# Transposing half of a stage's input by DMA instead of TensorE, at six places of a decoder trunk

## The chip, the cores and the metric

The kernel runs on one core of one Trainium2 chip. The metric is the device time of one execution in microseconds; lower is better.

## The reference

A decoder trunk of two layers on one sequence of 256 tokens, with 1024 features in float32. Each layer has a gated feed-forward network (FFN, 2816 hidden units), a token mixer and a second FFN. The first layer's mixer is a recurrent block, the second's is attention over keys and values that are computed once, from the residual between the layers. Every sub-layer has a norm in front and one behind:

```python
for layer in range(DEPTH):
    if layer == N_A_LAYERS:
        k, v, c = shared_kv(h, kv_norm_g, w_kv, w_fgate, b_fgate)
    f = swiglu(rms_norm(h, ffn1_pre_g[layer]), ...)
    h = h + 0.5 * rms_norm(f, ffn1_post_g[layer])
    hn = rms_norm(h, mix_pre_g[layer])
    m = recurrent_block(hn, ...) if layer < N_A_LAYERS else forgetting_attention(hn, w_q, w_o, k, v, c)
    h = h + rms_norm(m, mix_post_g[layer])
    f = swiglu(rms_norm(h, ffn2_pre_g[layer]), ...)
    h = h + 0.5 * rms_norm(f, ffn2_post_g[layer])
```

## The kernel before

**Blocks and units.** The 256 tokens are two blocks of 128, `t` = 0 and 1; the residual of a block is the tile `h[t]`, tokens on the partitions. All weights stream from memory through one list of units (`items`). A unit has a preparation, which loads the weights on SP's queue into one of five `raw` buffers and splits them into an upper and a lower float32r part (`split`: `whi` on ScalarE at L173, `wlo` on VectorE at L177, nine buffers of each), and a work part, once for each block, which is six matmuls of 512 columns for most units. A product is made of three matmuls, upper by upper, lower by upper and upper by lower, of weights and operands (L428, L429 and L432 in `proj_items`; L183 to L185 in `mm3`).

**Order.** TensorE's order is written by hand: `run` lets block 0 go up to seven units ahead of block 1. At the end of a stage block 0 finishes first, block 1 then does its last seven units alone, and block 0 starts the next stage with seven units alone. Each work part ends in a `tick`. `defer(n, fn)` calls `fn` at the (n+1)th tick from there, and so fixes where its TensorE instructions stand. The other engines' order is chosen at compile time from estimated readiness and priority; `tc.high_priority()` puts instructions forward, and `tc.keep_in_program_order` forbids one to stand before what was written ahead of it on its engine.

**From one stage to the next.** When a block's last product of a stage is done, `enter` takes the squares' sums (L205), multiplies by the norm's gain (L284), gets the reciprocal root on GpSimd (L198, L200) and adds to the residual in two halves of 512 features (L297). Then, `wait` ticks later, `inputs` makes the next stage's operand: `to_tp` transposes 128 x 128 tiles of the residual on TensorE (L226), four to a PSUM bank, two banks for eight feature tiles ("k tiles" 0 to 7); `to_x` multiplies them by the next norm's gain into `xg` (L234, VectorE), copies that rounded to the upper part `xhi` (L235, ScalarE) and takes the rest as the lower part `xlo` (L240, VectorE). `stat` takes the squares' sum of the new residual; the norm's factor itself is applied to the products later. The next stage's first unit uses k tiles 0 and 1, its second 2 and 3, its third 4 and 5.

`enter` is called at five changes of stage for both blocks. One makes its operand in another way (`normed`). Four use `inputs`: after the recurrent block, after the first layer's second FFN (where it makes two operands, `dests_l1`: one for the second layer's first FFN, one for the keys and values, whose names begin with z), after the second layer's first FFN, and after attention. After the last FFN nothing follows.

**Transposing transfers that are there already.** The hidden units of the FFN are transposed by DMA: `post_up` copies the float32 tile on GpSimd into two planes of 16-bit halves (L527), `hidden_T` issues a transposing DMA on SP's queue (L535) and a second copy on GpSimd joins the halves again (L540). The helpers `planes`, `swap` and `join` (L212, L216, L220) do the same for keys, queries and gates.

Of the kernel before, what the change touches and what calls it, by code (L numbers as in the profile page):

```python
# [9 lines left out]
F32 = mybir.dt.float32  # L10
# [7 lines left out]
P = 128  # L18
# [25 lines left out]
def trunk_kernel(ctx: ExitStack, tc: tile.TileContext, A: dict, out: bass.AP):  # L44
# [36 lines left out]
    def defer(n, fn):  # L81
        pend.append([n, fn])
# [146 lines left out]
    def x_upper(tp, dest, n):  # L229

        gi, xh, xl = dest
        xg = hpool.tile([P, 4, P], F32, tag="t1", name=nm("xg"), bufs=2)
        g = gT[:, gi + 4 * n:gi + 4 * n + 4].unsqueeze(2).to_broadcast([P, 4, P])
        nc.vector.tensor_tensor(xg, tp.rearrange("p (a b) -> p a b", a=4), g, ALU.mult)  # L234
        nc.scalar.activation(xh[:, 4 * n:4 * n + 4, :], xg, AF.Copy)  # L235
        return xg

    def x_lower(xg, dest, n):
        gi, xh, xl = dest
        nc.vector.tensor_tensor(xl[:, 4 * n:4 * n + 4, :], xg, xh[:, 4 * n:4 * n + 4, :].bitcast(F32), ALU.subtract)  # L240

    def to_x(tps, dest):

        with tc.high_priority():
            xg = [x_upper(tps[n], dest, n) for n in range(2)]
            for n in range(2):
                x_lower(xg[n], dest, n)

    def to_x_tiles(tps, dest):

# [15 lines left out]
    def stat(t):  # L266
        ss = new_ss()
        square_sum(h[t], ss[:, 0:1])
        rs[t] = rstd_of(ss, 1)

    def enter(t, dests, pf, gb, half, last=False, normed=False, wait=3):

        f = 1.0 / 16 if half else 1.0 / 32
        ss = new_ss()
        t1 = []
        urgent = tc.high_priority()
        urgent.__enter__()
        for n in range(2):
            square_sum(pf[n], ss[:, n:n + 1], f)
        for n in range(2):  # L280
            if n == 1 and last:
                r = rstd_of(ss, 2, f, nc.vector)
            t1.append(hpool.tile([P, 512], F32, tag="t1", name=nm("t1"), bufs=2))
            nc.vector.tensor_tensor(t1[n], pf[n], gb[:, n * 512:(n + 1) * 512], ALU.mult)  # L284
        if not last:
            r = rstd_of(ss, 2, f)

        sp, aq = nc.sync, nc.scalar
        pieces = [(n * 512, 512, None) for n in range(2)]
        if last:  # L290
            pieces = ([(0, 1024, sp)] if t == 0 else
                      [(0, 256, sp), (256, 256, aq), (512, 256, sp), (768, 256, aq)])
        for c, m, q in pieces:
            hn = h[t][:, c:c + m]
            for a in range(c, c + m, 512):
                n = min(m, 512)
                nc.vector.scalar_tensor_tensor(h[t][:, a:a + n], t1[a // 512][:, a % 512:a % 512 + n], r[:, 0:1],  # L297
                                               h[t][:, a:a + n], ALU.mult, ALU.add)
            if last:
                q.dma_start(out[0, t * P:(t + 1) * P, c:c + m], hn)  # L300
        urgent.__exit__(None, None, None)
        if last:
            return

        def inputs():
            tps = [to_tp(h[t], n) for n in range(2)]
            for dest in dests:
                to_x(tps, dest)
            stat(t)

        def norm():
            with tc.high_priority():
                normed_x()

        def normed_x():
            ss = new_ss()
            for n in range(2):
                square_sum(h[t][:, n * 512:(n + 1) * 512], ss[:, n:n + 1])
            rs[t] = rstd_of(ss, 2)
            hn = []  # L320
            for n in range(2):
                hn.append(hpool.tile([P, 512], F32, tag="t1", name=nm("hn"), bufs=2))
                nc.vector.tensor_scalar(hn[n], h[t][:, n * 512:(n + 1) * 512], rs[t][:, 0:1], None, ALU.mult)

            def go():
                tps = []
                for n in range(2):
                    tp = gtbank()
                    for j in range(4):
                        nc.tensor.transpose(tp[:, j * P:(j + 1) * P], hn[n][:, j * P:(j + 1) * P], ident)  # L330
                    tps.append(tp)
                to_x_tiles(tps, dests[0])
            defer(6, go)

        if normed:
            norm()
            settled[0] = True
        else:
            defer(wait, inputs)

    def gain_bcast(src):
        gb = hpool.tile([P, D], F32, tag="gb", name=nm("gb"), bufs=1)
# [149 lines left out]
    def ahead(i, fn):  # L492
# [5 lines left out]
            return prep()  # L498
        items[i] = (both, work)

    def ffn_items(pool_of, wg, wu, wd, post_g, next_dests, last=False, normed=False):
        hid = {}
        sil = {}
        box = {}

        def hid_tiles(t):
            if t not in hid:
                hid[t] = (pool_of().tile([P, 22, P], F32R, tag=f"hhi{t}", name=nm("hhi"), bufs=1),
                          pool_of().tile([P, 22, P], F32R, tag=f"hlo{t}", name=nm("hlo"), bufs=1))
            return hid[t]  # L510

        def post_gate(c0, nn):
            def f(t, ps):
                s = pool_of().tile([P, 512], F32, tag="sil", name=nm("sil"), bufs=2)
                nc.scalar.activation(s[:, :nn], ps, AF.Silu, scale=rs[t][:, 0:1])  # L515
                sil[t] = s
            return f

        def post_up(c0, nn):
            def f(t, ps):  # L520
                hh, hl = hid_tiles(t)
                s = sil[t][:, :nn]
                pr = pool_of().tile([P, 512], F32, tag="prod", name=nm("prod"), bufs=2)
                nc.vector.scalar_tensor_tensor(pr[:, :nn], ps, rs[t][:, 0:1], s, ALU.mult, ALU.mult)  # L524
                halves = hpool.tile([P, 512], F32, tag="t1", name=nm("pl"), bufs=2).bitcast(U16)[:, :2 * nn]
                turned = pr.bitcast(U16)[:, :2 * nn].rearrange("p (a b) -> p a b", b=P)
                nc.gpsimd.tensor_copy(halves.rearrange("p (h f) -> p h f", h=2),  # L527
                                      pr[:, :nn].bitcast(U16).rearrange("p (f h) -> p h f", h=2))
                defer(2, lambda: hidden_T(halves, turned, hh, hl))

            def hidden_T(halves, turned, hh, hl):

                m, k0 = nn // P, c0 // P
                keep = tc.keep_in_program_order
                keep(nc.sync.dma_start(turned, halves, transpose=True))  # L535
                hv = hh[:, k0:k0 + m, :].rearrange("p a b -> p (a b)")
                lv = hl[:, k0:k0 + m, :].rearrange("p a b -> p (a b)")

                def join():
                    nc.gpsimd.tensor_copy(halves.rearrange("p (f h) -> p h f", h=2),  # L540
                                          turned.rearrange("p (h a) b -> p h (a b)", h=2))

                def parts():
                    x = halves.bitcast(F32)
                    keep(nc.scalar.activation(hv, x, AF.Copy))  # L545
                    keep(nc.vector.tensor_tensor(lv, x, hv.bitcast(F32), ALU.subtract))  # L546
                defer(3, join)
                defer(7, parts)
            return f

        i0 = len(items)
        for i in range(5):
            proj_items(wg, i * 512, 512, main_x, post_gate(i * 512, 512))
            proj_items(wu, i * 512, 512, main_x, post_up(i * 512, 512))

        last_up = post_up(2560, 256)

        def post_both(t, pg, pu):
            post_gate(2560, 256)(t, pg)
            last_up(t, pu)  # L560

        pair_items(wg, wu, 2560, 256, main_x, post_both)

        def load_gb():
            box["gb"] = gain_bcast(post_g)

        ahead(i0 + 24, load_gb)

        def post_down(t, accs):
            enter(t, next_dests(t), accs, box["gb"], True, last, normed)  # L570

        row_items(wd, [P] * 22, lambda t, k: (hid[t][0][:, k, :], hid[t][1][:, k, :]), post_down, 4 if last else 2)
        return i0

# [644 lines left out]
    def post_q(n):  # L1219
        return lambda t, ps: heads_T(ps, t, n, HD ** -0.5, att["q"][t])  # L1220

    for n in range(2):
        proj_items(A["attn_w_q"][0], n * 512, 512, main_x, post_q(n))
    n_q[0] = len(items)
    row_items(A["attn_w_o"][0], [P] * 8, lambda t, k: (att["oh"][t][:, k, :], att["ol"][t][:, k, :]),
              lambda t, accs: enter(t, [main_dest(GI[("ffn2", 1)], t)], accs, gbox["mix1"], False, wait=4),
              rows0=1, late=True)
    ahead(n_q[0] + 2, load_gb("mix1", A["mix_post_g"][1]))
    n_att = len(items)
# [240 lines left out]
```

## Time and profile before

| | us |
|---|---|
| median of three runs | 965.7 |
| lowest and highest | 965.55, 965.88 |
| the profiled execution | 965.92 |
| its span, first to last instruction | 964.2 |
| TensorE busy | 955.9 |
| VectorE busy | 640.7 |
| ScalarE busy | 527.6 |
| GpSimd busy | 218.2 |

The granted clock of TensorE is 0.999 of full speed. Busy times are unions over one engine's instructions; the profile calls TensorE's matmuls PE and its weight loads PEld, VectorE DVE, ScalarE ACT, GpSimd POOL and the queue of SP SPq. Matmuls overlap each other in the pipeline, so the start of the next one tells more than the length of one. A row of the timeline gives the start and the duration in us, the engine, the line, the operation, the tiles written and read, their shapes, how many instructions are merged, and in brackets what ended the engine's idle time.

### The profile page before, as it was taken

The numbers are of one execution on the slowest core, as the hardware profiler recorded it, in microseconds if no ns is written. First come the engines' busy times: TensorE is split into PE (matmuls) and PEld (weight loads), VectorE is DVE, ScalarE is ACT, GpSimd is POOL, SyncE is SP. The second block draws the span as 40 slices with busy tenths as digits, with TensorE's granted clock in tenths as the row PEclk, the third lists the DMA queues.
The fourth block names the chain that finished last, engine by engine and source line by source line (L and its number), as shares of the span: only waits on it lengthen the run. The fifth ranks groups of instructions, "written<-read, shape, count | busy, mean of one in ns | idle before, by whom it ended". The sixth has DMA issues, their size and how long they took to land.

```text
span 964.2 us, 12866 instructions
## 1 busy us (share of the span) xinstructions
PE 955.9 (99%) x4575; PEld 791.3 (82%) x4575; DVE 640.7 (66%) x845; ACT 527.6 (55%) x750; POOL 218.2 (23%) x221
## 2 busy tenths in 40 slices
PE   9999999999999999999999999999999999999997
PEld 6888888898878888888898888888887788888886
DVE  6658674678997666664686566665488876666642
ACT  7546453568886555443565455444366855444431
POOL 2712330130001323230003522234022012232200
PEclk9999999999999999999999999999999999999999
DMA  8787995475346787775558979878773468777731
GB/s 286 226 258 225 256 284 197 142 228 163 119 123 219 209 236 211 205 242 196 135 182 278 253 219 258 230 216 265 226 256 97 133 199 236 207 222 233 223 109 44
DMA packets 148934, 198.79 MB, mean 206 GB/s; under 512 B 67166, under 2 KB 85958, under 8 KB 148742
## 3 DMA queue, kind: packets, MB, share of 16 engines
q1 hardware_dynamic: 146182, 191.06, 65.6%
q0 software_dynamic: 2080, 6.38, 2.1%
q8 instruction: 36, 0.59, 0.2%
q10 hardware_dynamic: 608, 0.53, 0.2%
q14 instruction: 28, 0.23, 0.1%
HBM read 182.19 MB, written 3.16 MB: 192 GB/s over the span
## 4 chain that ended last, share of the span: by engine, by line
PE 95%; DVE 2%; ACT 1%; issue 1%; POOL 0%; DMA 0%; POOLq 0%; DVEq 0%; ACTq 0%
PE mm L428 16%; PE mm L429 16%; PE mm L432 16%; PE mm L183 13%; PE mm L185 13%; PE mm L184 13%; PE gt L795 2%; PE mm L1305 1%; PE mm L190 1%; PE mm L191 1%; PE mm L192 1%; PE gt L226 1%; ACT pe L1181 1%; DVE wlo L177 0%; PE tr L127 0%
## 5 line engine op out<-in xcount | busy, mean ns | idle before, releaser
L177 DVE TENSOR_TENSOR wlo<-raw,whi 128x1024 fp32r<-128x1024 f32 (+5 forms) x329 | 418.0, 1276 | 230.7 <-ACT whi L173 228.3
L173 ACT ACTIVATE whi<-raw 128x1024 fp32r<-128x1024 f32 (+5 forms) x329 | 341.9, 1045 | 308.6 <-PE mm L432 119.2
L428 PE MATMUL mm<-whi,xhi 128*128 128x512 f32 x656 | 256.6, 391 | 0.0
L429 PE MATMUL mm<-wlo,xhi 128*128 128x512 f32 x656 | 255.5, 389 | 0.0
L432 PE MATMUL mm<-whi,xlo 128*128 128x512 f32 x656 | 202.1, 389 | 0.0
L428 PEld LDWEIGHTS mm<-whi,xhi 128*128 128x128 f32 x656 | 123.2, 188 | 25.9 <-issue 0.7
L432 PEld LDWEIGHTS mm<-whi,xlo 128*128 128x128 f32 x656 | 123.1, 188 | 25.8 <-DVE xlo L240 0.2
L429 PEld LDWEIGHTS mm<-wlo,xhi 128*128 128x128 f32 x656 | 123.2, 188 | 25.4 <-DVE wlo L177 0.3
L183 PE MATMUL mm<-whi,hhi 128*128 128x512 f32 x352 | 137.2, 390 | 0.0
L185 PE MATMUL mm<-whi,hlo 128*128 128x512 f32 x352 | 137.0, 389 | 0.0
L184 PE MATMUL mm<-wlo,hhi 128*128 128x512 f32 x352 | 136.9, 389 | 0.0
L540 POOL COPY pl<-prod 128x1024 uint16<-128x1024 uint16 (+1 forms) x48 | 69.9, 1456 | 174.4 <-DMA prod<-pl 174.4
L527 POOL COPY pl<-prod 128x1024 uint16<-128x1024 uint16 (+1 forms) x48 | 66.3, 1382 | 151.9 <-DVE prod L524 86.8
L183 PEld LDWEIGHTS mm<-whi,hhi 128*128 128x128 f32 x352 | 66.1, 188 | 13.7
L185 PEld LDWEIGHTS mm<-whi,hlo 128*128 128x128 f32 x352 | 66.1, 188 | 13.7
L184 PEld LDWEIGHTS mm<-wlo,hhi 128*128 128x128 f32 x352 | 66.1, 188 | 13.6
L198 POOL TENSOR_SCALAR nv<-ss 128x1 f32<-128x1 f32 x22 | 9.6, 437 | 268.7 <-ACT junk L205 268.7
L524 DVE SCALAR_TENSOR_TENSOR prod<-mm,rstd,sil 128x512 f32<-128x512 f32 (+1 forms) x48 | 33.8, 703 | 29.5 <-PE mm L432 25.9
L515 ACT ACTIVATE sil<-mm,rstd 128x512 f32<-128x512 f32 (+1 forms) x48 | 31.0, 649 | 32.9 <-PE mm L432 25.0
L546 DVE TENSOR_TENSOR hlo<-pl,hhi 128x512 fp32r<-128x512 f32 (+1 forms) x48 | 41.2, 858 | 3.7 <-ACT hhi L545 3.7
L183 PE MATMUL mm<-whi,xhi 128*128 128x512 f32 (+1 forms) x112 | 42.8, 382 | 0.0
L185 PE MATMUL mm<-whi,xlo 128*128 128x512 f32 (+1 forms) x112 | 42.5, 379 | 0.0
(223 smaller groups left out, 1054.6 us busy)
## 6 DMA issues: line engine op xcount, KB each, us to landing
raw<-in_ffn_w_down_dram SPq DMA_DIRECT2D x88, 512.0 KB
raw<-in_ffn_w_up_dram SPq DMA_DIRECT2D x80, 512.0 KB
raw<-in_ffn_w_gate_dram SPq DMA_DIRECT2D x78, 512.0 KB
raw<-in_rg_w_in_dram SPq DMA_DIRECT2D x10, 504.0 KB
raw<-in_rg_w_out_dram SPq DMA_DIRECT2D x10, 504.0 KB
raw<-in_ffn_w_gate_dram SPq DMA_DIRECT2D x19, 256.0 KB
raw<-in_ffn_w_up_dram SPq DMA_DIRECT2D x16, 256.0 KB
raw<-in_rg_w_in_dram SPq DMA_DIRECT2D x8, 512.0 KB
```

What stands on the lines that cost most here:

```text
L173: up = nc.scalar.activation(hi[:parts, c:c + m], rawv[:, c:c + m], AF.Copy)
L177: nc.vector.tensor_tensor(lo[:parts, c:c + m], rawv[:, c:c + m], hi[:parts, c:c + m].bitcast(F32), ALU.subtract)
L183: nc.tensor.matmul(ps, xh, wh, start=first, stop=False)
L184: nc.tensor.matmul(ps, xh, wl, start=False, stop=False)
L185: nc.tensor.matmul(ps, xl, wh, start=False, stop=last)
L428: nc.tensor.matmul(ps, get_x(t, k)[0], u.hi[:, c], start=k == 0, stop=False)
L429: nc.tensor.matmul(ps, get_x(t, k)[0], u.lo[:, c], start=False, stop=False)
L432: nc.tensor.matmul(ps, get_x(t, k)[1], u.hi[:, c], start=False, stop=k == nk - 1)
L524: nc.vector.scalar_tensor_tensor(pr[:, :nn], ps, rs[t][:, 0:1], s, ALU.mult, ALU.mult)
L527: nc.gpsimd.tensor_copy(halves.rearrange("p (h f) -> p h f", h=2), pr[:, :nn].bitcast(U16).rearrange("p (f h) -> p h f", h=2))
L540: nc.gpsimd.tensor_copy(halves.rearrange("p (f h) -> p h f", h=2), turned.rearrange("p (h a) b -> p h (a b)", h=2))
L546: keep(nc.vector.tensor_tensor(lv, x, hv.bitcast(F32), ALU.subtract))
```

## The change

At six of the eight uses of `inputs` the second half of the residual (k tiles 4 to 7) is transposed by a transposing DMA: after the recurrent block for block 1, after the first layer's second FFN for both blocks, after the second layer's first FFN for block 0, and after attention for both. `enter` copies the half into planes (`planes`, GpSimd) as soon as the residual is added. `inputs` transposes only the first half on TensorE, sets the first half of the first operand, and issues the transfer (`swap`, SP); `join` (GpSimd) follows at the next tick, and one tick after that (two for block 1) `turned_to_x` sets the second half: the product with the gain on VectorE and the upper part on ScalarE, both kept in program order, and the lower part. A second operand (keys and values) is set three ticks later, both halves. For block 1 at these places `inputs` comes one tick later than before.

The scratch tiles are old product tiles of the FFN (block 0 behind an FFN), the query tile of block 0 (behind attention), and for block 1 one of the two `t1` tiles and the tile that takes the squares in `stat` (`junk`).

```diff
     def to_x(tps, dest):
         with tc.high_priority():
-            xg = [x_upper(tps[n], dest, n) for n in range(2)]
-            for n in range(2):
-                x_lower(xg[n], dest, n)
+            xg = [x_upper(tp, dest, n) for n, tp in enumerate(tps)]
+            for n, v in enumerate(xg):
+                x_lower(v, dest, n)
+
+    def turned_to_x(v, tps, dests, more):
+        for i, dest in enumerate(dests):
+            def place(i=i, dest=dest):
+                gi, xh, xl = dest
+                if i:
+                    to_x(tps, dest)
+                with tc.high_priority():
+                    xg = (v if i == len(dests) - 1 else more()).rearrange("p (a b) -> p a b", a=4)
+                    g = gT[:, gi + 4:gi + 8].unsqueeze(2).to_broadcast([P, 4, P])
+                    tc.keep_in_program_order(
+                        nc.vector.tensor_tensor(xg, v.rearrange("p (a b) -> p a b", a=4), g, ALU.mult))
+                    tc.keep_in_program_order(nc.scalar.activation(xh[:, 4:, :], xg, AF.Copy))
+                    x_lower(xg, dest, 1)
+            if i:
+                defer(2, place)
+            else:
+                place()
...
+        by_transfer = not normed and (spare or t == 1) and not (half and len(dests) == 1 and t == 1)
+        if by_transfer:
+            a = spare() if t == 0 else hpool.tile([P, 512], F32, tag="t1", name=nm("hp"), bufs=2)
+            with tc.high_priority():
+                planes(a.bitcast(U16), h[t][:, 512:])
+
         def inputs():
-            tps = [to_tp(h[t], n) for n in range(2)]
-            for dest in dests:
+            tps = [to_tp(h[t], n) for n in range(1 if by_transfer else 2)]
+            for dest in dests[:1] if by_transfer else dests:
                 to_x(tps, dest)
             stat(t)
+            if by_transfer:
+                b = spare() if t == 0 else spool.tile([P, 512], F32, tag="junk", name=nm("ht"), bufs=1)
+                with tc.high_priority():
+                    swap(b.bitcast(U16), a.bitcast(U16))
+                defer(0, lambda: join(a.bitcast(U16).rearrange("p (f h) -> p h f", h=2), b.bitcast(U16)))
+                defer(1 + t, lambda: turned_to_x(a, tps, dests, spare))
...
-            defer(wait, inputs)
+            defer(wait + (by_transfer and t), inputs)
...
+    def old_products():
+        return pools["f"].tile([P, 512], F32, tag="prod", name=nm("hp"), bufs=2)
...
+    q_parts = [1, 0]
+
+    def old_q():
+        return att["q"][0].rearrange("p a b -> p (a b)").rearrange("p (s f) -> p s f", s=2)[:, q_parts.pop(), :]
```

`spare=old_products` is passed behind the FFNs and `spare=old_q` behind attention; the recurrent block's call passes none.

More of the change, by code (lines that the diff above doesn't have):

```diff
@@ L269, in stat, with enter @@
         rs[t] = rstd_of(ss, 1)
-    def enter(t, dests, pf, gb, half, last=False, normed=False, wait=3):
+    def enter(t, dests, pf, gb, half, last=False, normed=False, wait=3, spare=None):
         f = 1.0 / 16 if half else 1.0 / 32
@@ L569, in post_down @@
         def post_down(t, accs):
-            enter(t, next_dests(t), accs, box["gb"], True, last, normed)
+            enter(t, next_dests(t), accs, box["gb"], True, last, normed, spare=old_products)
         row_items(wd, [P] * 22, lambda t, k: (hid[t][0][:, k, :], hid[t][1][:, k, :]), post_down, 4 if last else 2)
@@ L1225, in trunk_kernel @@
     row_items(A["attn_w_o"][0], [P] * 8, lambda t, k: (att["oh"][t][:, k, :], att["ol"][t][:, k, :]),
-              lambda t, accs: enter(t, [main_dest(GI[("ffn2", 1)], t)], accs, gbox["mix1"], False, wait=4),
+              lambda t, accs: enter(t, [main_dest(GI[("ffn2", 1)], t)], accs, gbox["mix1"], False, wait=4,
+                                    spare=old_q),
               rows0=1, late=True)
```

## The prediction

> **What bounds the kernel now.** I read the page first, then the waits of TensorE, then the instructions grouped by form, and last the timeline around each place that is changed.
>
> ```profile
> span 964.2 us, 12866 instructions
> ...
> PE 955.9 (99%) x4575; PEld 791.3 (82%) x4575; DVE 640.7 (66%) x845; ACT 527.6 (55%) x750; POOL 218.2 (23%) x221
> ...
> PE 95%; DVE 2%; ACT 1%; issue 1%; POOL 0%; DMA 0%; POOLq 0%; DVEq 0%; ACTq 0%
> ```
>
> TensorE is busy for 99% of the span and carries 95% of the chain that ended last. Busy matmul time overlaps, so I also ask what TensorE ever waited for:
>
> ```profile
> PE tr L127 <- PEq L1455: 0.8, 1, 0.8
> PE gt L795 <- issue: 0.8, 1, 0.8
> PE gt L1165 <- POOL qT L220: 0.3, 1, 0.3
> ```
>
> That is 1.9 us in three waits, none of them at the six places. So a TensorE instruction that goes is worth its full step, and a new wait of TensorE costs its full length. The other engines matter only when they are late.
>
> **Part one: what is removed.** Each of the six places loses four of its eight transposes, 24 of these 64 (group view: number, busy us, mean ns of one, idle before).
>
> ```profile
> L226 PE MATMUL gt<-ident,h 128*128 128x128 f32 x64 | 8.3, 272 | 0.0
> ```
>
> ```profile
> 303.67 0.39 PE L429 MATMUL mm<-wlo,xhi 128*128 128x512 f32 x1
> 303.90 0.62 PE L432 MATMUL mm<-whi,xlo 128*128 128x512 f32 x2
> 304.36 1.03 PE L226 MATMUL gt<-ident,h 128*128 128x128 f32 x8
> 305.15 0.48 PE L428 MATMUL mm<-whi,xhi 128*128 128x512 f32 x1
> ```
>
> The eight in a group start in a pipeline: they last 1.03 us together, each 0.272, so they step by (1.03 - 0.272)/7 = 0.108 us. Four fewer save 0.43 us, and six places save 24 x 0.108 = 2.6 us. The other end comes from the group's busy time, 8.3/64 = 0.130 us, which gives 3.1 us; that counts the group's run-out too, which stays, so I take 2.6. [...]
>
> VectorE's and ScalarE's instructions stay the same in number and size:
>
> ```profile
> L234 DVE TENSOR_TENSOR xg<-gt,gT 128x512 f32<-128x512 f32 x20 | 12.8, 683 | 0.1
> ...
> L235 ACT ACTIVATE xhi<-xg 128x512 fp32r<-128x512 f32 x16 | 9.8, 631 | 4.3 <-DVE xg L234 4.3
> ```
>
> The second half's product with the gains (L234) now reads SBUF instead of PSUM. I price that at nothing: the weight split in a row below reads two SBUF operands of twice the length in 1226 ns, 613 for this length against 683.
>
> **Part two: what is added.** Per place there are a de-interleaving copy on GpSimd, a transposing transfer on SP's queue and a re-joining copy on GpSimd: 12 copies and six transfers. The kernel already does the same for the hidden units, and one such case reads:
>
> ```profile
> 315.36 1.04 POOL L527 COPY pl<-prod 128x1024 uint16<-128x1024 uint16 x1 [8.62 <-DVE prod L524]
> 320.04 1.36 POOL L540 COPY pl<-prod 128x1024 uint16<-128x1024 uint16 x1 [3.64 <-DMA prod<-pl]
> ```
>
> ```profile
> 316.42 1.24 SPq L535 DMA_TRANSPOSE prod<-pl  x1
> ```
>
> ```profile
> POOL pl L540 <- DMA prod<-pl: 174.4, 46, 10.1
> ```
>
> From the residual's end the second half needs 1.04 (copy) + 0.02 + 3.62 (316.42 to 320.04) + 1.36 (copy) + 0.68 + 0.63 = 7.35 us until its upper part can be used. The waits for landing average 174.4/46 = 3.8, and the longest was 10.1. Against this stands the room, from the second half of the residual to the first matmul on k tile 4, which is the third unit of the next stage (units of two k tiles, six matmuls). In order of the six places, each residual pair with the matmul that follows:
>
> ```profile
> 303.10 1.42 DVE L297 SCALAR_TENSOR_TENSOR h<-t,rstd,h 128x512 f32<-128x512 f32 x2 [0.31 <-POOL rstd L200]
> 316.13 0.39 PE L428 MATMUL mm<-whi,xhi 128*128 128x512 f32 x1
> 473.20 1.41 DVE L297 SCALAR_TENSOR_TENSOR h<-t,rstd,h 128x512 f32<-128x512 f32 x2 [0.36 <-POOL rstd L200]
> 484.31 0.39 PE L428 MATMUL mm<-whi,xhi 128*128 128x512 f32 x1
> 484.44 1.40 DVE L297 SCALAR_TENSOR_TENSOR h<-t,rstd,h 128x512 f32<-128x512 f32 x2
> 495.53 0.39 PE L428 MATMUL mm<-whi,xhi 128*128 128x512 f32 x1
> 701.11 1.41 DVE L297 SCALAR_TENSOR_TENSOR h<-t,rstd,h 128x512 f32<-128x512 f32 x2 [0.38 <-POOL rstd L200]
> 712.19 0.39 PE L428 MATMUL mm<-whi,xhi 128*128 128x512 f32 x1
> ```
>
> ```profile
> 779.82 1.42 DVE L297 SCALAR_TENSOR_TENSOR h<-t,rstd,h 128x512 f32<-128x512 f32 x2 [0.24 <-POOL rstd L200]
> 793.40 0.39 PE L428 MATMUL mm<-whi,xhi 128*128 128x512 f32 x1
> ```
>
> The rooms are 316.13 - 304.52 = 11.6, 484.31 - 474.61 = 9.7, 495.53 - 485.84 = 9.7, 712.19 - 702.52 = 9.7 and, for the last place, 793.40 - 781.24 = 12.2; the fifth place, not shown, is block 0 of the same stage as the sixth, and I treat it like that one. Each room shrinks by the 0.43 saved in front of it, so three places have 9.3 against 7.35: a margin of 1.9. In front of the second half there can stand one weight split on VectorE, 1.2 (1226 ns in a row below), and one on ScalarE, 1.3 (an estimate, twice L235's 0.63 for twice its length). With both, the second half comes 9.85 us after the residual, 0.55 late. With a landing slower by 0.2 (3.8 for 3.6) and two copies of 1.54 for 1.04 and 1.36 (rows below), the sum is 10.7 and 1.4 late. So a tight place costs between nothing and 1.4 us; I take 0.17, near the lower end, because the plain chain fits with 1.9 to spare and the new instructions have priority over the splits: 0.5 us over three places. The first, fifth and sixth places I cost at nothing: their room is 2 to 2.5 us longer, which covers the 1.4.
>
> **Part three: what is moved.** The second block's transposes come one unit later, at its three places. What covers this is the rest of the run of block 0's units in between; a unit is 1.4 us (six steps of 0.23, from 303.67 to 303.90), and the group then lasts 0.272 + 3 x 0.108 = 0.6 instead of 1.03. I cost it at nothing, and at 0 to 0.5 per place if VectorE is late. It also gains something: a residual that VectorE finishes late no longer meets TensorE at once. The keys' and values' operands are set later; their first use is four units after.
>
> **Part four: what is queued behind the new waits.** On SP the six transfers wait for their first copy, and weight loads stand behind: 1.24 us each plus the wait. The loads run ahead of their use by five buffers, so this is hidden. On GpSimd the joining copy waits for the landing, and behind it stands the row statistic of the next block. On VectorE and ScalarE the gain product and the upper part are pinned in program order; behind them stand the weight splits, the evictions and the next block's residual. The stage where this hurts is the entry to the second layer, with both blocks and two sets of operands:
>
> ```profile
> 474.50:494.00 19.50, 19.50 (x103) 16.95 (x102) 19.31 (x29) 13.63 (x24) 2.95 (x6) 1.00 0.46 142
> ```
>
> ```profile
> 491.00 0.86 DVE L177 TENSOR_TENSOR wlo<-raw,whi 128x680 fp32r<-128x680 f32 x1
> 494.61 0.31 PE L183 MATMUL mm<-whi,zhi 128*128 128x340 f32 x1
> ```
>
> VectorE (the third pair) is busy 19.31 of 19.50 us there. The first split of 680 columns ends at 491.86, and its first matmul is at 494.61: the weights are 2.75 us ahead. The change puts four copies of GpSimd into this stretch, and they slow VectorE. Two windows of the by-form view, the first without copies, the second with 13:
>
> ```profile
> L177 DVE TENSOR_TENSOR wlo<-raw,whi 128x1024 fp32r<-128x1024 f32 x10 | 12.3, 1226 | 14.6 <-ACT whi L173 14.6
> ```
>
> ```profile
> L177 DVE TENSOR_TENSOR wlo<-raw,whi 128x1024 fp32r<-128x1024 f32 x27 | 36.2, 1339 | 17.9 <-ACT whi L173 17.5 <-DMA raw<-in_ffn_w_up_dram 0.4
> ...
> L527 POOL COPY pl<-prod 128x1024 uint16<-128x1024 uint16 x7 | 10.7, 1532 | 28.8 <-ACT hhi L545 17.9 <-DVE prod L524 11.0
> ...
> L540 POOL COPY pl<-prod 128x1024 uint16<-128x1024 uint16 x6 | 9.3, 1546 | 21.4 <-DMA prod<-pl 21.4
> ```
>
> 27 splits lost 113 ns each, 3.1 us over 13 copies: 0.23 us of VectorE for a copy, 0.9 us for four, inside the 2.75. [...]
>
> **The sum** is made against the profiled execution's 965.9 us (span 964.2 and 1.7 around it): 2.6 saved, 0.5 given back, 2.1 net, 963.8. That execution lies 0.2 above the median of 965.7, so against the median it is **963.6 us**.
>
> **The rivals.** *The second half is late.* Each tight place loses the 1.4 us of the upper bound: 965.7 - 2.6 + 4.2 = 967.3; with half of it, 965.2. For it speaks the margin of 1.9, which two splits ahead use up; against it the priority.
>
> *VectorE stands still and the weights run out (the slower side).* The pinned product waits at the head of VectorE's queue. At the second place it is queued two units behind the transposes, so 2.8 us or more after the residual, while the joining copy ends 1.04 + 0.02 + 3.62 + 1.36 = 6.04 after it: VectorE may idle up to 3.2 us. The third place can do the same, 6.4 together, and 0.9 for the copies makes 7.3. It decides once this passes the lead of 2.75: TensorE then waits up to 4.6 us, and the time is 965.7 - 2.6 + 4.6 = 967.7, or 971.9 with the 4.2 of the late halves on top. For it speaks the 19.31 of 19.50; against it that VectorE's order is chosen by readiness as the compiler expects it, and that the second block's operands for the keys and values now come later, which takes 4 x 0.68 = 2.7 us out of the tight stretch.
>
> [...]
>
> *The change does not do what it says*: the transposes taken out might have filled time in which TensorE would wait anyway. The 1.9 us of waits lie elsewhere, so 2 in 100; the time would be 965.7.
>
> **How the numbers follow.** A measurement of this kernel can tell about 0.2%, 1.9 us, from no change: 963.8 and 967.6 are the bounds. The forecast has 0.52 and ends below 963.8. The late second half has 0.22, and lies within the bounds. The stand-still has 0.20 and lies past 967.6. Exclusion has 0.04 and no effect 0.02, both within. So faster 0.52, same 0.28, slower 0.20. The range runs from 962.9, with 2.6 saved and nothing given back, rounded down by the spread of the runs, to 967.5, which leaves out the stand-still.
>
> **What would show it.** In the changed profile L226 would have 40 matmuls instead of 64, the groups at the six places four each; GpSimd 12 more copies of about 1.0 to 1.5 us; the transposing transfers six more at about 1.24. TensorE's waits would stay near 1.9 us, or show the upper part (the place's ScalarE line) at k tile 4 for the late half, and weight splits (L177) in the second layer's entry for the stand-still. I am wrong on the first term if the groups of four take more than about 0.6 us, and on the second if any of the three tight places shows TensorE waiting for more than 1 us.

## The result, and the profile after

| | before | after |
|---|---|---|
| median of six runs, us | 965.71 | 970.65 |
| lowest and highest, us | 965.55, 966.06 | 969.74, 973.3 |
| mean granted clock of TensorE in the runs | 0.998 to 1.0 | 0.995 to 0.997 |

The changed kernel is slower: after to before 1.0052, 95% interval 1.0041 to 1.0062. It takes 4.9 us more, where the forecast had 2.1 us less. The time lies above the forecast's range and inside the slower rival's 967.7 to 971.9, but that is chance: the rival is added up from waits of TensorE for late weights and for the late halves, and the trace below has 0.3 us of these. The execution that was profiled is the slowest of the six (973.3). Of the 7.4 us by which its span is longer, 1.9 lie ahead of every changed place: its first transposes of the residual (L226) start at 298.36, before at 296.47.

The head of the page of the changed kernel and its chain (columns as before):

```profile
span 971.6 us, 12835 instructions
...
PE 958.9 (99%) x4551; PEld 792.0 (82%) x4551; DVE 647.9 (67%) x845; ACT 527.5 (54%) x750; POOL 244.5 (25%) x233
...
PE 91%; DVE 2%; ACT 2%; issue 2%; DMA 1%; POOL 1%; POOLq 0%; ACTq 0%; DVEq 0%
```

TensorE is as good as always busy in both, and lost 24 instructions, yet its busy time is 3 us longer (958.9 for 955.9): some of its matmuls got longer. The chain gave 4 points of TensorE to other engines, so there are new waits. TensorE's waits in the changed kernel (total us, times, longest):

```profile
PE mm L183 <- ACT zhi L235: 2.0, 1, 2.0
PE gt L226 <- DVE h L316: 0.9, 2, 0.5
PE gt L829 <- issue: 0.8, 1, 0.8
PE tr L127 <- PEq L1495: 0.8, 1, 0.8
PE mm L1345 <- DVE whi L1312: 0.5, 1, 0.5
PE mm L463 <- DVE xlo L240: 0.3, 1, 0.3
PE gt L1199 <- POOL qT L220: 0.2, 1, 0.2
```

Of the waits over 0.2 us, the two of 0.8 were there before. The one of 0.5 for `whi` L1312 lies in the kernel's first unit, ahead of every place changed. It belongs to this execution rather than to the change: one variant below shows no such wait, another one of 0.8. The other three rows, 3.2 us, are new, and they lie at two of the four changes of stage: 2.4 us come from the entry to layer 2's first FFN, where both blocks have a transfer (L183 and one of the two for L226), and 0.9 from the change of stage behind that FFN, where only block 0 has one (L463 and the other for L226). Each has its row below.

Four groups of instructions, by form (busy us, mean ns, idle before):

```profile
L212 POOL COPY hp<-h 128x1024 uint16<-128x1024 uint16 x5 | 9.5, 1895 | 7.6 <-DVE h L316 7.6
L226 PE MATMUL gt<-ident,h 128*128 128x128 f32 x40 | 6.0, 276 | 1.0 <-DVE h L316 0.9
...
L260 DVE TENSOR_TENSOR hp<-hp,gT 128x512 f32<-128x512 f32 x7 | 4.8, 689 | 8.9 <-POOL hp L220 8.9
...
L261 ACT ACTIVATE xhi<-hp 128x512 fp32r<-128x512 f32 x5 | 3.1, 630 | 12.9 <-DVE hp L260 12.9
```

The 24 transposes are gone, 64 to 40. The copies into planes took 1.9 us on average, where the forecast had 1.04 for its plain chain and 1.54 for its worst one. VectorE stood 8.9 us in front of the gain product of a transferred half, and ScalarE 12.9 us in front of its upper part. Where nothing urgent waits behind them, such idle times showed no loss: the kernel below with transfers behind the mixers alone is 0.8 us faster than the kernel before. At the entry to layer 2's first FFN something does. The timeline there (start, duration, engine, line; in brackets the idle time before):

```profile
475.36 0.75 DVE L316 SCALAR_TENSOR_TENSOR h<-t,rstd,h 128x512 f32<-128x512 f32 x1
...
476.17 1.97 POOL L212 COPY hp<-h 128x1024 uint16<-128x1024 uint16 x1 [1.51 <-DVE h L316]
...
481.28 2.05 POOL L220 COPY hp<-hp 128x1024 uint16<-128x1024 uint16 x1 [1.33 <-DMA hp<-hp]
...
483.36 0.69 DVE L260 TENSOR_TENSOR hp<-hp,gT 128x512 f32<-128x512 f32 x1 [1.24 <-POOL hp L220]
...
484.08 0.64 ACT L261 ACTIVATE xhi<-hp 128x512 fp32r<-128x512 f32 x1 [2.21 <-DVE hp L260]
...
484.62 0.58 ACT L205 ACTIVATE junk<-mm 128x512 bf16<-128x512 f32 x1
...
487.77 1.42 DVE L316 SCALAR_TENSOR_TENSOR h<-t,rstd,h 128x512 f32<-128x512 f32 x2 [0.24 <-POOL rstd L200]
488.58 0.65 PE L226 MATMUL gt<-ident,h 128*128 128x128 f32 x4 [0.34 <-DVE h L316]
...
490.60 0.63 ACT L235 ACTIVATE zhi<-xg 128x512 fp32r<-128x512 f32 x1 [0.17 <-DVE xg L234]
...
491.28 0.67 PE L183 MATMUL mm<-whi,zhi 128*128 128x360 f32 x1 [2.05 <-ACT zhi L235]
```

The same stretch of the kernel before:

```profile
480.74 0.63 ACT L235 ACTIVATE zhi<-xg 128x512 fp32r<-128x512 f32 x1 [0.60 <-DVE xg L234]
481.27 0.58 ACT L205 ACTIVATE junk<-mm 128x512 bf16<-128x512 f32 x1
...
487.93 0.32 PE L183 MATMUL mm<-whi,zhi 128*128 128x360 f32 x1
```

Block 0's residual ended at 474.61 before and ends at 476.11 now, so 1.5 us are to be taken off the later times. ScalarE now stands 2.21 us in front of block 0's upper part (L261), and behind it in its queue are the squares of block 1's layer entry (L205): 484.62 - 1.5 = 483.1 against 481.27, 1.9 us late. Block 1's residual ends at 489.19 - 1.5 = 487.7 against 485.84, also 1.9 late, and TensorE waits 0.34 us for it. The keys' and values' operand of block 0 (`zhi`), ready 480.74 + 0.63 = 481.37 and first used at 487.93 before, comes behind all this at 491.23: TensorE waits 2.05 us. The chain of work that ended last runs the same way: the first copy, the transfer, the second copy, L260, L261, the squares, block 1's residual, `zhi`.

From shortly before the end of that wait the granted clock is lower (0.88 over 490:491, 1.00 over 489:490). Busy us of the engines by window (PE, PEld, DVE, ACT, POOL), then the granted clock, DMA share and GB/s:

```profile
489.00:495.00 6.00, 3.95 (x15) 3.49 (x13) 5.11 (x9) 3.53 (x6) 2.62 (x4) 0.65 0.73 228
495.00:500.00 5.00, 5.00 (x22) 4.65 (x21) 3.19 (x6) 2.42 (x4) 1.09 (x1) 0.74 0.00 0
```

The low value is 0.5: the windows 491:492, 492:493, 494:495 and 496:497 each show 0.50. So 0.65 over 6 us and 0.74 over 5 us are (0.35 x 6 + 0.26 x 5)/0.5 = 6.8 us at half clock, which cost 3.4 us. No wait stands for this in the list; it is in the longer busy time: one matmul of 360 columns starts 0.30 us after the other there (from 492.48 on), 0.16 in the kernel before (from 487.93 on).

Behind layer 2's first FFN, where only block 0 has a transfer, block 1 is late too (the last row counts seven of the eight transposes, since the stretch that is shown ends there):

```profile
711.02 1.24 SPq L216 DMA_TRANSPOSE hp<-hp  x1
...
712.35 0.53 SPq L161 DMA_DIRECT2D raw<-in_attn_w_q_dram  x1
...
714.13 1.50 POOL L220 COPY hp<-hp 128x1024 uint16<-128x1024 uint16 x1 [1.32 <-DMA hp<-hp]
...
714.33 2.31 DVE L177 TENSOR_TENSOR wlo<-raw,whi 128x1024 fp32r<-128x1024 f32 x1
...
716.36 1.06 ACT L173 ACTIVATE whi<-raw 128x1024 fp32r<-128x1024 f32 x1 [0.56 <-DMA raw<-in_attn_w_q_dram]
...
717.17 1.21 DVE L177 TENSOR_TENSOR wlo<-raw,whi 128x1024 fp32r<-128x1024 f32 x1
...
719.63 0.73 PE L463 MATMUL mm<-whi,xlo 128*128 128x512 f32 x2 [0.34 <-DVE xlo L240]
...
720.90 1.27 PE L226 MATMUL gt<-ident,h 128*128 128x128 f32 x7 [0.53 <-DVE h L316]
```

A weight split that starts while GpSimd's joining copy runs takes 2.31 us; one without takes 1.21. The copy ends at 715.63, and from there to the split's end at 716.64 are 1.0 us, not far from its usual length: by my estimate from these times it had done 0.2 us of its work (1.21 - 1.0) in the 1.3 beside the copy. Behind it stand the lower part of the transferred half and block 1's residual, and TensorE waits for both.

A second delay is on SP's queue. The load of the query weights (`in_attn_w_q`) starts 0.1 us behind the transfer's 1.24 us, and 712.35 - 708.96 = 3.4 us after block 0's residual. In the kernel before it starts 1.2 us after it (703.69 - 702.52). So the transfer, which starts 0.03 us after its copy has ended (709.02 + 1.97 = 710.99) and stands in the queue ahead of the load, holds it back by 2.2 us, and ScalarE waits 0.56 us for these weights ahead of the upper part (L261) and of block 1's squares. The kernel before doesn't show this wait.

### The profile page after: what moved, and what is told of

It is laid out like the page before. It is cut to its first block, busy times and chain, and to the rows that moved or that the text cites. A ratio compares the mean times of both kernels' runs of the same rounds, so it can differ in the third digit from the quotient of the medians.

```text
span 971.6 us, 12835 instructions
## 1 busy us (share of the span) xinstructions
PE 958.9 (99%) x4551; PEld 792.0 (82%) x4551; DVE 647.9 (67%) x845; ACT 527.5 (54%) x750; POOL 244.5 (25%) x233
## 4 chain that ended last, share of the span: by engine, by line
PE 91%; DVE 2%; ACT 2%; issue 2%; DMA 1%; POOL 1%; POOLq 0%; ACTq 0%; DVEq 0%
PE mm L459 16%; PE mm L460 15%; PE mm L463 15%; PE mm L183 12%; PE mm L185 12%; PE mm L184 12%; PE gt L829 2%; PE mm L1345 1%; PE mm L190 1%; PE mm L191 1%; PE mm L192 1%; ACT pe L1215 1%; DVE wlo L177 1%; DVE h L316 0%; ACT junk L205 0%
## 5 line engine op out<-in xcount | busy, mean ns | idle before, releaser
L177 DVE TENSOR_TENSOR wlo<-raw,whi 128x1024 fp32r<-128x1024 f32 (+5 forms) x329 | 425.2, 1298 | 216.6 <-ACT whi L173 215.4
L463 PE MATMUL mm<-whi,xlo 128*128 128x512 f32 x656 | 202.3, 389 | 0.3 <-DVE xlo L240 0.3
L463 PEld LDWEIGHTS mm<-whi,xlo 128*128 128x128 f32 x656 | 123.0, 188 | 26.7 <-DVE xlo L240 1.0
L183 PE MATMUL mm<-whi,hhi 128*128 128x512 f32 x352 | 137.2, 390 | 0.0
L574 POOL COPY pl<-prod 128x1024 uint16<-128x1024 uint16 (+1 forms) x48 | 70.9, 1477 | 172.5 <-DMA prod<-pl 172.4
L561 POOL COPY pl<-prod 128x1024 uint16<-128x1024 uint16 (+1 forms) x48 | 68.0, 1416 | 138.1 <-DVE prod L558 75.6
L183 PEld LDWEIGHTS mm<-whi,hhi 128*128 128x128 f32 x352 | 66.1, 188 | 13.7
L183 PE MATMUL mm<-whi,xhi 128*128 128x512 f32 (+1 forms) x112 | 42.8, 382 | 0.0
```

The lines of the kernel that those rows point to most:

```text
L177: nc.vector.tensor_tensor(lo[:parts, c:c + m], rawv[:, c:c + m], hi[:parts, c:c + m].bitcast(F32), ALU.subtract)
L183: nc.tensor.matmul(ps, xh, wh, start=first, stop=False)
L463: nc.tensor.matmul(ps, get_x(t, k)[1], u.hi[:, c], start=False, stop=k == nk - 1)
```

## The experiments

Theory 1: a transferred half of block 0 costs time where block 1's layer entry (its `enter`) follows at once, since its pinned and lengthened steps stand on VectorE and ScalarE ahead of block 1's residual and of what else is due. The half clock comes on top, from the wait. Rivals: the transfers cost everywhere; the late operands of the keys and values do it by themselves; the copies, beside which VectorE's splits take longer (2.31 us for 1.21), do it by themselves. All were timed in five rounds beside the kernel before. Its median was 965.98 us beside the three kernels that split the places and the one with the operands in time, 966.23 beside the one for ScalarE's part, and 965.83 beside the other four. Differences below are between medians; the ratios, with their 95% intervals, are not taken from the medians, and what they give differs by up to 0.8 us.

**Where it is lost.** Three kernels split the six places among them, by the condition alone:

```diff
+ e1: by_transfer = not normed and (spare or t == 1) and not half
+ e2: by_transfer = not normed and len(dests) == 2
+ e3: by_transfer = not normed and half and len(dests) == 1 and t == 0
```

> The transfers only at the three places behind the mixers (recurrent block for block 1, attention for both blocks); behind the FFNs all is as before. Theory 1 (the loss lies at the entry to the second layer, and a smaller one behind the second layer's first FFN): the three places keep what the trace of the changed kernel shows of them, -0.48, -0.46 and -0.51 us, so 965.7 - 1.45 = 964.3. Theory 2 (the twelve copies on GpSimd each cost the same share of the loss, by keeping VectorE out): the loss of 4.9 us and the 2.6 saved make 7.5 over 12 copies, 0.63 each; six copies and half of the saving make 965.7 - 1.3 + 3.8 = 968.2.

Measured: 965.19 us (964.63 to 965.55), ratio 0.9987 (0.9978 to 0.9996), 0.8 us gained. The forecast's saving for three places is 3 x 0.43 = 1.3 us; the interval, 0.4 to 2.1 us, holds both.

> The transfers only at the entry to the second layer, where each block has two operands. Theory 1: nearly the whole loss, +5.35 - 0.31 = +5.0 us of the changed kernel's trace, so 970.7, with a wait of TensorE of some 2 us for the keys' and values' operand of block 0 and a granted clock of one half for some 7 us behind it. Theory 2: four copies, 965.7 - 0.9 + 2.5 = 967.3.

Measured: 970.27 us (968.52 to 971.27), ratio 1.0036 (1.0024 to 1.0049). TensorE's waits show the same 2.0 us:

```profile
PE mm L183 <- ACT zhi L235: 2.0, 1, 2.0
```

Its five runs fall in two groups: 968.52 and 968.89 us at a mean clock of 0.998, and 970.27 to 971.27 at 0.995 to 0.996. The profiled one is of the first group and has the wait without the half clock. So without the half clock these two places cost 968.7 - 966.0 = 2.7 us, after what their missing transposes save, and the half clock, where it comes, about 2 more.

> The transfer only behind the second layer's first FFN, for block 0. Theory 1: -0.41 + 1.69 = +1.3 us, 967.0, because the upper part of the transferred half stands on ScalarE in front of the squares of block 1, whose residual then comes late for its transposes. Theory 2: two copies, 965.7 - 0.4 + 1.25 = 966.5.

Measured: 967.59 us (967.18 to 968.2), ratio 1.0015 (1.0006 to 1.0023), 1.6 us lost. Its trace has TensorE waiting for block 1's residual, longer than in the changed kernel:

```profile
PE gt L226 <- DVE h L316: 0.9, 1, 0.9
```

The late load is there again, and here the chain of work that ended last runs through it: ScalarE waits 0.88 us for the weights, then come the upper part and block 1's squares.

```profile
710.12 1.06 ACT L173 ACTIVATE whi<-raw 128x1024 fp32r<-128x1024 f32 x1 [0.88 <-DMA raw<-in_attn_w_q_dram]
...
711.09 0.61 ACT L261 ACTIVATE xhi<-hp 128x512 fp32r<-128x512 f32 x1
...
711.61 0.58 ACT L205 ACTIVATE junk<-mm 128x512 bf16<-128x512 f32 x1
```

So at this place theory 1 names only a part of the cause; how the 1.6 us divide between the late weights and the longer splits isn't shown.

The three together are -0.8 + 1.6 + 4.3 = 5.1 us against the change's 4.9: within the noise the places add up, and the whole loss sits in three of the six.

**Which of the blocks.** The changed kernel without the two transfers of block 0 behind which block 1 follows; block 1 in front of layer 2's first FFN keeps its transfer and late operands (the expectation's "layer 1's entry" counts layers from 0 there; its "feed forward of layer 2" is the place behind that FFN).

```diff
- (spare or t == 1) and not (half and len(dests) == 1 and t == 1)
+ (spare or t == 1) and (not half or (len(dests) == 2 and t == 1))
```

> The changed kernel with the transfers at four of the six places: not for block 0 in front of layer 1's entry and not for block 0 in front of the feed forward of layer 2, the two places behind which block 1's layer entry follows at once. Block 1 in front of layer 1's entry keeps its transfer and its late operands. Theory 1 (only a transferred half that stands in front of another block's layer entry costs): 964.2 to 965.4 us, 0.43 less than with the transfers at the three other places alone (965.19), no wait above 0.6 us at the layer entry. Theory 2 (every transfer at the layer entry costs, through its copies or its late operands): 966.2 to 968.5 us.

Measured: 964.91 us (964.78 to 965.41), ratio 0.9991 (0.9982 to 1.0000), in theory 1's range. None of TensorE's new waits over 0.2 us is left, and its transposes show the four groups saved:

```profile
L226 PE MATMUL gt<-ident,h 128*128 128x128 f32 x48 | 6.5, 272 | 0.0
```

So block 1's transfer there, with its copies and its late operands, costs nothing that can be seen, while block 0's two, with block 0's late operands, turned a gain of 0.9 us into a loss of 4.9. This is the best version run. Against the kernel before it is 0.1% faster, within the 0.2% that I take for no change; that it beats the kernel with transfers behind the mixers alone (965.19) isn't shown.

**Late operands by themselves.** The kernel before, with only the second operand deferred as in the change:

```diff
-            for dest in dests:
-                to_x(tps, dest)
+            to_x(tps, dests[0])
             stat(t)
+            if len(dests) == 2:
+                defer(4 + t, lambda: to_x(tps, dests[1]))
```

> The kernel before with one edit: at the two layer entries the keys' and values' operands are made four units later for block 0 and five for block 1, as they are late in the changed kernel; no transposing transfer anywhere. Theory 1 (what costs the time at the layer entry is the work of the transferred half, which stands on ScalarE and VectorE ahead of block 1's layer entry, and everything behind it comes late whatever its order): without that work the late operands cost little, 965.8 to 966.6 us, against 965.98 for the kernel before. Theory 2 (making these operands late is by itself what opens the wait of 2.2 us on them): 968 to 970.5 us, with a wait of about 2 us of TensorE for zhi.

Measured: 966.59 us (966.38 to 966.75), ratio 1.0006 (0.9997 to 1.0014): 0.8 us, at the upper end of theory 1's range, far from theory 2's. The interval, -0.3 to 1.4 us, doesn't exclude zero, though all eleven runs lie above 26 of the 28 beside them. The trace has one new wait, for a bank of transposes that VectorE empties late:

```profile
PE gt L226 <- DVE xg L234: 0.3, 1, 0.3
```

**The operands in time, the transfers kept.** The changed kernel, with the first half of the keys' and values' operand set at once:

```diff
-            for dest in dests[:1] if by_transfer else dests:
+            for dest in dests:
...
-                if i:
-                    to_x(tps, dest)
```

> The changed kernel, but the first half of the keys' and values' operand is set together with the first half of the other operand, before the transfer; only its second half is set three ticks later. Theory 1a (what TensorE waits for is that operand's late place in the order): the wait of 2.2 us and the half clock behind it (2.6 us) go, 970.65 - 4.8 = 965.9. Theory 1b (ScalarE and VectorE stand still for the transferred half, and everything behind is late whatever the order): the wait moves to another operand of that entry, 968 to 971.

Measured: 970.26 us (969.71 to 971.81), ratio 1.0043 (1.0029 to 1.0056). The wait for the first half is gone, and others have come in its place: the second half of the same operand (L259 is L261 here), its lower part, block 1's residual.

```profile
PE mm L183 <- ACT zhi L259: 1.5, 1, 1.5
...
PE mm L185 <- DVE zlo L240: 0.7, 1, 0.7
PE gt L226 <- DVE h L314: 0.5, 1, 0.5
```

So the order of the two operands isn't the cause. Everything behind the transferred half is late, and whatever is due first shows it. Four of the five runs have a mean clock of 0.998 or 0.999, the profiled one among them: here the 4.3 us come nearly without the half clock.

**The copies by themselves.** The kernel before with the change's twelve GpSimd copies and their tiles, results unused, no transfer, operands as before:

```diff
+            with tc.high_priority():
+                planes(a.bitcast(U16), h[t][:, 512:])
...
+                defer(1, lambda: join(b.bitcast(U16).rearrange("p (f h) -> p h f", h=2), a.bitcast(U16)))
```

> The kernel before with the twelve GpSimd copies of the change added, with their tiles and about where they stand, their results used by nothing; no transposing transfer, all transposes on TensorE, operands as before. Theory 1 (the loss is the order at the two tight places; a copy that holds up VectorE costs only where a layer entry is close): 965.9 to 967.2 us. Theory 2 (the copies' exclusion of VectorE, about 0.8 to 1.1 us for each copy that falls on a long VectorE instruction, is itself the loss): 969 to 973 us, with waits of 0.5 us and more at the layer entry and behind the first half of the feed forward.

Measured: 966.85 us (966.34 to 968.5), ratio 1.0011 (1.0002 to 1.0019): 1.0 us for all twelve. The first copies are as long as in the changed kernel:

```profile
L212 POOL COPY hp<-h 128x1024 uint16<-128x1024 uint16 x5 | 9.5, 1904 | 7.8 <-DVE h L297 7.8
```

The splits are longer here too, 382.3 us for the 292 of 1024 columns where the kernel before takes 378.2, but by themselves the copies cost little.

**ScalarE's part.** The changed kernel with the upper part of the transferred half made by VectorE, so that ScalarE doesn't stand in front of the squares:

```diff
-   tc.keep_in_program_order(nc.scalar.activation(xh[:, 4:, :], xg, AF.Copy))
+   tc.keep_in_program_order(nc.vector.tensor_copy(xh[:, 4:, :], xg))
```

> The changed kernel with one edit: the upper part of the transferred half is made by VectorE, right behind its gain product, in place of ScalarE, so that ScalarE no longer stands 2.2 us in front of block 1's squares. Theory 1a (ScalarE's stand is the larger part of the delay at the layer entry): block 1's residual comes 0.9 to 1.2 us earlier, TensorE's wait for zhi falls from 2.0 to 1.2 us or less, the clock keeps its full value (0.998 to 0.999), and the time is 967.0 to 968.6 us. Theory 1b (VectorE, which stands for the same product and gets one more instruction, carries the delay as well): the wait for zhi stays at 1.7 us or more, with 969.0 to 971.0 us.

Measured: 970.0 us (968.87 to 970.82), ratio 1.0036 (1.0024 to 1.0048). The timeline of the same stretch, whose times are 2.3 us ahead of the changed kernel's (the joining copy starts at 478.98 here and at 481.28 there):

```profile
481.06 0.69 DVE L260 TENSOR_TENSOR hp<-hp,gT 128x512 f32<-128x512 f32 x1 [1.24 <-POOL hp L220]
...
481.79 0.58 ACT L205 ACTIVATE junk<-mm 128x512 bf16<-128x512 f32 x1
...
484.63 1.40 DVE L316 SCALAR_TENSOR_TENSOR h<-t,rstd,h 128x512 f32<-128x512 f32 x2
...
488.17 0.43 PE L183 MATMUL mm<-whi,zhi 128*128 128x360 f32 x1 [1.45 <-ACT zhi L235]
```

Block 1's residual ends at 486.03, which is 0.9 us earlier than in the changed kernel once the 2.3 are put back, and the wait for `zhi` falls from 2.05 to 1.45. Neither theory is met in full: of the 1.9 us by which block 1 is late, ScalarE's stand is about half. New waits of 0.4 us come in for the upper part, which VectorE now makes, and for `zlo`. The loss against the kernel before fell from 4.9 to 3.8 us (the intervals, 4.0 to 6.0 and 2.3 to 4.6, overlap), and part of that is the clock, whose mean is 0.996 in only three of the six runs and 0.998 in the others. VectorE still stands 1.24 us for the same product.

**The half clock.** The changed kernel with ten matmuls without use where TensorE waits for `zhi`:

```diff
                 if k0 == 0:
                     acc[t] = mmbank()
+                    if extra and t == 0:
+                        keep_busy(10)
```

> The changed kernel with one edit: ten matmuls without use (about 2.1 us on TensorE) stand ahead of the first values' unit of block 0, in the place of the 2.2 us in which TensorE waits for zhi. Theory 1 (that wait is what drops the clock to half for 6.8 us): no half clock behind it, a mean clock of 0.998 to 0.999 in place of 0.995 to 0.997, and 968.3 to 969.8 us. Theory 2 (the drop of the clock has nothing to do with the wait): a mean clock of 0.995 to 0.997 still, and 970.0 to 972.0 us.

Measured: 968.82 us (968.7 to 969.09), ratio 1.003 (1.0018 to 1.0041). All six runs have a mean clock of 0.998 or 0.999, against 0.995 to 0.997 in all six of the changed kernel. The same windows as above:

```profile
489.00:495.00 6.00, 5.87 (x32) 4.91 (x30) 4.58 (x8) 2.63 (x5) 1.99 (x3) 1.00 0.44 106
495.00:500.00 5.00, 5.00 (x26) 4.32 (x25) 4.12 (x10) 3.27 (x8) 0.00 (x0) 1.00 0.04 6
```

With ten matmuls more the median is 1.8 us lower; against the kernel before in each comparison the loss fell from 4.9 to 3.0 us, 1.9 less. That the clock drops from the wait is shown. The 1.9 us are less than the 3.4 that the profile's 6.8 us at half clock cost, but that profile is of the slowest run. The profile of the kernel for ScalarE's part has a clock of 0.83 over 485:495, which is 0.17 x 10/0.5 = 3.4 us at half clock and 1.7 us lost, nearer to it.

## Why the prediction was wrong

The step that failed is the zero that the sum has for parts three and four, for what stands behind the new steps on VectorE, ScalarE and SP. Block 0's two transfers behind the FFNs, with its late operands, cost 5.8 us (from -0.9 to 4.9): the traces show block 1's work late behind them and TensorE waiting, and 1.9 of the 5.8 is the clock, which the prediction didn't have at all.

**Part one held in kind.** 40 transposes are left, a group of four takes 0.60 us as forecast, and with transfers at four of the six places TensorE waits for nothing new. The kernel with transfers at three places gained 0.8 us and the one with four 0.9, where 3 and 4 times 0.43 are 1.3 and 1.7. By the medians about half of the saving is given back by something that I did not locate; the intervals (0.4 to 2.1 and 0 to 1.7 us) reach up to the full saving.

**Part two failed at its length.** The second half was to be usable 7.35 us after the residual, 9.85 at worst. At the entry to layer 2's first FFN it takes 484.72 - 476.11 = 8.6 us, inside the bounds but 1.3 longer than the plain chain, with 0.9 more in the first copy (1.97 for 1.04), 0.7 more in the second (2.05 for 1.36) and 0.5 less between them (3.14 for 3.64). TensorE waited for it at only one place, 0.3 us. The term I took, 0.5 us, was of the right size. The sign that I had named, a wait of more than 1 us at a tight place, did come, but it was a wait for the other operand and not for the late half.

**Part three had the late operands at nothing.** Their first use is four units after, and I counted TensorE's order only. Deferring them alone costs 0.8 us at the median; with the transfers in place the slack is gone, 487.93 - 481.37 = 6.6 us between ready and used before and a wait of 2.05 now. What decides is when VectorE and ScalarE reach them, and in the timeline block 1's late residual stands ahead of them there. The second block's later transposes, the other zero of this part, cost nothing that can be seen in the kernel with four transfers, which has them at all three places.

**Part four saw the place and took the wrong victim.** I named the pinned product, and the next block's residual behind it, but in the rival I let the weights run out. TensorE's list has no wait for a split (L177), so at the entry the lead of the weights held. VectorE stood 1.24 us and not up to 3.2; ScalarE, which I had not priced, stood 2.21. The victims were the squares, the residual and the operands of the *other* block, and the place's price was 2.7 us without the clock. On SP I took the weight loads behind the transfers as hidden. Behind the FFN they weren't: the load came 2.2 us late, and ScalarE waited 0.56 us for it in the changed kernel and 0.88 in the one with this transfer alone.

**The price of a copy, 0.23 us, was an average over the wrong rows.** 13 copies among 27 splits in a stretch where VectorE stood 17.9 us in front of its splits say what a copy costs where it meets little. A copy that meets a long split costs VectorE 2.31 - 1.21 = 1.1 us, and the copies grow to 1.9. The split of 714.33 did by my estimate 0.2 us of its work in the 1.3 beside the copy. Exclusion, which has 0.04 in the prediction, was not shown; what the runs show is this 1.1 us for a split beside a copy of 1.50, and 1.0 us for all twelve copies by themselves, where the sum has nothing for them.

**The clock was missing altogether.** I priced a wait of TensorE at its length. This one cost 1.9 us more, by the filled wait. The profile of the changed kernel has 6.8 us at half clock behind a wait of 2.05 us, and that of the kernel with transfers at the layer entry alone has a wait of 2.05 us, too, and a clock of 1.00 over 489:495. What decides between the two was not shown.

Added up: -0.9 for the four harmless places, +1.6 behind layer 2's first FFN, +2.7 for its entry without the clock and +1.9 for the clock are 5.3 against 4.9 measured; block 1 of the entry is in the first term and in the third. Open remains how the 2.7 us divide among the stands of VectorE and ScalarE, the lengthened splits and the deferred operands: single parts give 0.8 (operands) and 1.0 (all copies), ScalarE's stand 1.1 with its effect on the clock (4.9 less 3.8, within the noise), and they needn't add. No run has the transfers without the pinned order, so what the pins alone cost isn't shown.

## What to carry to other kernels

Before an instruction is pinned that waits for a DMA, list what stands behind it on its engine up to the next thing that TensorE needs, the other block's work included, and do the same for the DMA's own queue: that list, not the slack of the data itself, is the price. When TensorE is the bound, 0.43 us of its time per place isn't worth 7 us of latency on two engines unless the place has nothing following closely; decide place by place, since four of the six here cost nothing and two turned the whole into a loss. Price two engines that hold each other up from instructions that met (here a split of 2.31 us for 1.21 and a copy of 1.97 for 1.04), one by one, not from a mean over a stretch, and price a wait of TensorE of about 2 us with the clock that it may drop (here 1.9 us more).

## What the runs showed of the hardware that I had not expected

- A wait of TensorE of 2.05 us, 0.34 us of waiting shortly ahead of it, was followed by 6.8 us at half clock in the changed kernel's profile; the same two waits in the profile of the kernel with transfers at the layer entry alone were not. In its five runs the mean clock says that three had it, worth about 2 us each. Length alone doesn't decide: a wait of 1.45 us was followed by 3.4 us at half clock in the kernel for ScalarE's part; the profiled execution of the kernel with the operands in time has one of 1.5 and a mean clock of 0.999.
- Ten useless matmuls in that wait lower the median by 1.8 us.
- A copy of GpSimd (16-bit, 1024 per partition) took 1.97 us where VectorE was splitting weights; a split that met a copy took 2.31 us instead of 1.21.
- A transposing transfer that waited on SP's queue for its copy held the weight load behind it back by 2.2 us: 3.4 us after the residual instead of 1.2.
